# Hymba layer on one core: the zero rows beside the decode tokens written to DRAM ahead of time

## The chip, the cores and the metric

The kernel runs on one core of a Trainium2 chip. The metric is the device time of one execution in microseconds, the median of several runs.

## The reference

One layer of a hybrid decoder in its inference step, in float32, for 2,048 prompt tokens (one sequence) and 8 decode tokens (one of each of 8 sequences), with a model width of 2,048. What is computed, cut to what matters:

```python
shift, scale, gate = adaln(c, w_c, b_c)
h = rmsnorm(x, g_pre) * (1.0 + scale) + shift
u_a, v_a, z_a, x_b, z_b = split(h @ w_in)              # five parts of 1024 columns
y_a = u_a * chunk_mix(layernorm(v_a), w_s, b_s) * silu(z_a)
y_b, h_re, h_im = s5_branch(x_b, h0, ...)              # diagonal state-space scan, 64 groups of 16 channels
y_b = y_b * silu(z_b)
out = x + gate * rmsnorm(concat([y_a, y_b]) @ w_out, g_post)
```

The outputs are `out` for prompt and decode tokens, the decode tokens' normalised `v_a`, and the S5 states of both.

## The kernel before, in words

**Arithmetic.** Every large matrix product is made of three float32 products on TensorE (`mm3`, lines 97 to 99): operand and weight are each split into a high and a low part, and high-high, high-low and low-high are summed. A weight piece of 128 x 1024 is loaded by SyncE (`wraw`, L108), ScalarE casts its high half (`whi`, L90), and VectorE or GpSimd subtracts to get the low half (`wlo`, L85). Weights are loaded one column tile ahead.

**Tiles and stages.** Tokens go in four blocks `b` of 512 (the last has the 8 decode tokens besides, in two ranges of 256 and 264 tokens, `ranges`, L58). In the first part every block computes 16 column tiles of 128 columns: 8 of `x_b` and 8 of `z_b`, with 16 steps of k each. The loop over blocks (L1449 to L1470) starts a block with `group_start`, which makes the normalised input of the block from x, its row factor `R` and the shift (L373 to L375), and goes on with `phase1_rest` (L570), which calls `half(i, hf)` before each half of a column tile. `half` advances generators by a step: the statistics of the next block (`stats`: an x load L329, two squares on ScalarE L335 and L337, an addition on GpSimd L338, sixteen times two k tiles, and then `rms_wide`, which gives `R` by a Newton iteration on VectorE, L140 to L145), the matrices of the S5 branch (`s5_mats`: GpSimd products L810 to L812 for E, F and `bb`, ScalarE casts such as `qh` L883, transposes and small products on TensorE), and the gate of the ada layer (L271 to L291). The accumulators of the column tiles are PSUM tiles `acc`, in a ring of four banks.

**The stores that the change is about.** The results of a column tile `e` go to DRAM in chunks of 8 tokens, time-major, for the S5 scan that follows: `XB[e]` has for each of 128 columns, 8 times `t` and 2 halves (high, low) a row of 272 numbers, `ZB[e]` for each `t` and column a row of 264. The 256 prompt chunks lie in the middle, the 8 decode sequences beside them: in front (`0:ND`) and at the end (`ND+NK:XW`) of `XB`'s rows, and at the end of `ZB`'s. A decode token fills one of the eight times; the other seven are zero. `ev_xb` (L391 to L415) and `ev_zb` (L417 to L432) evict a tile, and in the last block write the decode part too: GpSimd sets a tile `dz` to zero (L409, L429), VectorE (and ScalarE in `ev_zb`) writes the token's numbers into it (L412, L413, L430, L431), and SyncE stores the whole, zeros and all (L414, L415, L432). Each number row of 8 float32 is a packet of 32 B: 2,048 packets for each of the two `XB` stores of a tile, 1,024 for the `ZB` store. `dz` has two buffers.

**What sets the order.** The code is written in the order of the loops above, and a scheduler that simulates the engines then sets the order on each engine; so a transfer need not stand where the loop yields it. Each engine, SyncE's queue of transfers among them, works in its order.

Of the kernel before, what the change touches and what calls it, by code (L numbers as in the profile page):

```python
# [11 lines left out]
F32 = mybir.dt.float32  # L12
F32R = mybir.dt.float32r
I32 = mybir.dt.int32
AF = mybir.ActivationFunctionType
# [6 lines left out]
ND = 8  # L22
# [5 lines left out]
G = 64  # L28
# [3 lines left out]
TC = 8  # L32
NK = L // TC
XW = NK + 2 * ND
HW = NK + ND
EPS = 1e-6
NE = 8
# [20 lines left out]
def ranges(b):  # L58

    return [(0, TB)] if b < NB - 1 else [(0, 256), (256, 264)]  # L60


class Builder:
# [330 lines left out]
    def ev_xb(self, b, e, acc):  # L394

        hi, lo = self.tile_(), self.tile_()
        hv, lv = (o[:, 0:TB].rearrange("p (t k) -> p t k", t=TC) for o in (hi, lo))
        for a, (r0, rn) in zip(acc, ranges(b)):
            m = min(rn, TB - r0)
            av = a[:, 0:m].rearrange("p (k t) -> p t k", t=TC)  # L400
            ks = slice(r0 // TC, (r0 + m) // TC)
            self.S.copy(hv[:, :, ks].bitcast(F32R), av)
            self.sub(self.V, lv[:, :, ks].bitcast(F32R), av, hv[:, :, ks])
        cols = slice(ND + b * 64, ND + b * 64 + 64)
        self.SP.dma_start(self.XB[e][:, :, 0, cols], hv)
        self.SP.dma_start(self.XB[e][:, :, 1, cols], lv)
        if b == NB - 1:
            dz = self.sp_.tile([128, 2, TC, 2, ND], F32, tag="dz", bufs=2, name=self.nm("dz"))
            self.G.memset(dz, 0.0)  # L409
            d = acc[1][:, 256:264]  # L410
            for i, t in ((0, TC - 1), (1, 0)):
                self.V.tensor_copy(dz[:, i, t, 0, :].bitcast(F32R), d)  # L412
                self.sub(self.V, dz[:, i, t, 1, :].bitcast(F32R), d, dz[:, i, t, 0, :])  # L413
            self.SP.dma_start(self.XB[e][:, :, :, 0:ND], dz[:, 0])  # L414
            self.SP.dma_start(self.XB[e][:, :, :, ND + NK : XW], dz[:, 1])  # L415

    def ev_zb(self, b, e, acc):  # L417
        o = self.tile_()
        ov = o[:, 0:TB].rearrange("p (t k) -> p t k", t=TC)
        for a, (r0, rn) in zip(acc, ranges(b)):  # L420
            m = min(rn, TB - r0)
            av = a[:, 0:m].rearrange("p (k t) -> p t k", t=TC)
            os_ = ov[:, :, r0 // TC : (r0 + m) // TC]
            self.S.activation(os_, av, AF.Sigmoid)
            self.V.tensor_mul(os_, os_, av)
        self.SP.dma_start(self.ZB[e].rearrange("t p k -> p t k")[:, :, b * 64 : b * 64 + 64], ov)
        if b == NB - 1:
            dz = self.sp_.tile([128, 2, TC, ND], F32, tag="dz", bufs=2, name=self.nm("dz"))
            self.G.memset(dz[:, 0], 0.0)  # L429
            self.S.activation(dz[:, 0, 0, :], acc[1][:, 256:264], AF.Sigmoid)  # L430
            self.V.tensor_mul(dz[:, 0, 0, :], dz[:, 0, 0, :], acc[1][:, 256:264])  # L431
            self.SP.dma_start(self.ZB[e].rearrange("t p k -> p t k")[:, :, NK:HW], dz[:, 0])  # L432

    def ev_v(self, b, j, acc):
        T, V, S = self.T, self.V, self.S
# [941 lines left out]
    def build(self):  # L1377
        nc, tc, I, V, G, SP = self.nc, self.tc, self.I, self.V, self.G, self.SP
# [29 lines left out]
        with tc.manual_schedule():  # L1408
            w, acc = self.startup(st, NG, nta)
# [19 lines left out]
        def mats_step():  # L1429

            paced[0] += 1
            while paced[1] * n_a < paced[0] * (8 * NE + 2):
                paced[1] += 1
                next(mats, None)
        def stats(b):

            n = blk(b)
            ssq = self.xp.tile([128, TB + ND], F32, tag="ssq", bufs=1, name=self.nm("ssq"))
            for i in range(KT):
                self.stat_add(self.xp, self.xload(self.xp, "xst", b, i, 2), ssq, i, n, G)  # L1440
                yield 1
            self.rms_wide(ssq, n, self.R[b])
            if n > TB:
                self.hdec(self.R[b])
        pair = lambda ntl: lambda hf: [self.wsplit(self.wpair(I["win"], ntl[1][0], 0))] if hf else []
        half1 = lambda ntl, i: lambda hf: self.wsplit(self.whalf(I["win"][ntl[1][i]], hf))


        for b in range(NB):  # L1449
            st_ = stats(b + 1) if b + 1 < NB else iter(())  # L1450
            if b:
                w = self.group_start(b, nta, w[0], self.R[b], half1(nta, 2))
            def half(i, hf, b=b, st_=st_):
                if i >= 3:
                    next(st_, None)
                if b == 0 and i == 8 and hf == 0:
                    self.s5_lanes(pp)
                if (b or i > 8) and i < len(nta[0]) - 1:
                    mats_step()
                if b and hf:  # L1460
                    next(gate, None)
                return (), ()
            w = self.phase1_rest(b, nta, 2 if b else NG, half, w, pair(nta) if b + 1 < NB else half1(ntb, 0))
            for _ in st_:
                pass
# [20 lines left out]
        for b in (NB - 1, *range(NB - 1)):  # L1486
            if b < NB - 1:
                w = self.v_tokens(b, w[0], self.R[b], half, ntb[1][8])
            if b != NB - 2:
                w = self.phase1_rest(b, ntb, 8 if b < NB - 1 else 0, half, w, lambda hf: [self.vpair(0)] if hf else [])  # L1490
            else:
                y0, ws0 = [], []
                raws = []
                def last(k):

                    if k == 1:
                        raws.extend(self.wraw(self.wpair(I["wout"], g, 0)) for g in (0, 2))
                    if k in (9, 14):
                        ws0.extend(self.wpieces(raws.pop(0)))
                    if k >= 4 and k % 2 == 0:  # L1500
                        y0.append(self.yload(0, len(y0)))
                self.phase1_rest(b, ntb, 8, half, w, lambda hf: [], last)
# [94 lines left out]
```

## Time and profile before

| | |
|---|---|
| median of 3 runs | 2885.63 us |
| lowest, highest | 2882.94, 2888.16 us |
| the profiled execution's own time | 2882.97 us |
| its span, first to last instruction | 2880.9 us |
| mean granted TensorE clock | 0.994 |
| busy share of VectorE, ScalarE, GpSimd | 55%, 37%, 36% |
| DRAM traffic | 466.94 MB read, 102.66 MB written |

The profile shows one execution on the core. Times are from the span's start. Block 0's column tiles run until about 270 us, blocks 1 and 2 until about 690, and block 3, where the decode part is stored, from about 690 to 900 us. The rest of the time goes to the v, z, u tiles, the S5 scan and the output projection, which the change does not touch.

### The profile page before, as it was taken

To read this page: it belongs to the slowest core of one execution; us is meant where nothing else is said; L and a number is where in the kernel's file an instruction comes from. 1 tells how busy PE (TensorE), PEld (TensorE's weight loads), DVE (VectorE), ACT (ScalarE), POOL (GpSimd) and SP (SyncE) were. 2 spreads that over 40 slices of the span, in tenths; PEclk is the share of its full clock that TensorE was granted. 3 is DMA by queue.
4 is the path that set the end of the run, shared out by engine and by line. 5 is a ranking of instruction groups with operands and counts; after the bars stand their busy time and mean duration, and the time that the engine had idled before them with its cause. 6 is when DMAs were issued, how large, how long until landed. Compare 5 with 4: busy or idle time off the path is not lost.

```text
span 2880.9 us, 44125 instructions
## 1 busy us (share of the span) xinstructions
PE 2817.2 (98%) x15708; PEld 2365.8 (82%) x15708; DVE 1570.4 (55%) x2907; ACT 1062.2 (37%) x2008; POOL 1048.5 (36%) x973
## 2 busy tenths in 40 slices
PE   7999999999999999999999999999999999999998
PEld 4676777778899999988888888888888888888976
DVE  4467656465342837564647545573641273472866
ACT  3334444334233232423233332433243333434543
POOL 1128562662431233323232323233334355263442
PEclk9999999999999999999999999999999999999999
DMA  9898997987987373847475656646573355464676
GB/s 363 287 250 230 265 261 229 282 234 210 198 209 207 106 236 125 267 131 223 133 245 185 180 174 196 209 145 208 159 229 106 112 178 171 132 219 126 197 235 221
DMA packets 455167, 581.20 MB, mean 202 GB/s; under 512 B 216609, under 2 KB 303265, under 8 KB 454945
## 3 DMA queue, kind: packets, MB, share of 16 engines
q1 hardware_dynamic: 454946, 578.38, 66.9%
q8 instruction: 123, 2.02, 0.3%
q14 instruction: 98, 0.80, 0.1%
HBM read 466.94 MB, written 102.66 MB: 198 GB/s over the span
## 4 chain that ended last, share of the span: by engine, by line
PE 73%; DVE 14%; DMA 6%; issue 3%; POOL 1%; SPq 1%; ACT 1%; DVEq 0%; ACTq 0%; POOLq 0%
PE acc L97 21%; PE acc L99 20%; PE acc L98 20%; DVE Ub L943 3%; DVE wlo L85 2%; PE acc L655 2%; PE acc L656 2%; PE acc L657 2%; PE ada L271 1%; DMA wraw<-in_win 1%; DVE Ub L954 1%; DVE sct L953 1%; DVE sct L951 1%; DVE Ub L952 1%; DMA wraw<-in_woutr 1%
## 5 line engine op out<-in xcount | busy, mean ns | idle before, releaser
L85 DVE TENSOR_TENSOR wlo<-wraw,whi 128x512 fp32r<-128x512 f32 x626 | 544.6, 878 | 832.9 <-ACT whi L90 811.8
L90 ACT CAST whi<-wraw 128x512 fp32r<-128x512 f32 x960 | 580.4, 620 | 1101.3 <-PE acc L98 634.8
L97 PE MATMUL acc<-hi,whi 128*128 128x512 f32 (+2 forms) x2816 | 979.2, 349 | 1.4 <-ACT vtok L663 0.8
L99 PE MATMUL acc<-hi,wlo 128*128 128x512 f32 (+2 forms) x2816 | 968.7, 344 | 4.0 <-DVE wlo L85 3.9
L98 PE MATMUL acc<-lo,whi 128*128 128x512 f32 (+2 forms) x2816 | 968.2, 344 | 3.8 <-DVE lo L375 3.5
L85 POOL TENSOR_TENSOR wlo<-wraw,whi 128x512 fp32r<-128x512 f32 x334 | 472.7, 1418 | 1025.0 <-ACT whi L90 911.8
L97 PEld LDWEIGHTS acc<-hi,whi 128*128 128x128 f32 x2816 | 531.1, 189 | 82.2 <-issue 14.0
L99 PEld LDWEIGHTS acc<-hi,wlo 128*128 128x128 f32 x2816 | 530.4, 188 | 74.0 <-DVE wlo L85 6.1
L98 PEld LDWEIGHTS acc<-lo,whi 128*128 128x128 f32 x2816 | 531.1, 189 | 65.0 <-DVE lo L375 6.7
L97 PE MATMUL acc<-yhi,whi 128*128 128x512 f32 (+1 forms) x1024 | 377.3, 369 | 3.8 <-DVE o L1118 2.8
L99 PE MATMUL acc<-yhi,wlo 128*128 128x512 f32 (+1 forms) x1024 | 375.5, 368 | 2.1 <-POOL wlo L85 2.1
L98 PE MATMUL acc<-ylo,whi 128*128 128x512 f32 (+1 forms) x1024 | 376.1, 368 | 0.0
L97 PEld LDWEIGHTS acc<-yhi,whi 128*128 128x128 f32 x1024 | 193.5, 189 | 39.6 <-DVE o L1118 3.6
L99 PEld LDWEIGHTS acc<-yhi,wlo 128*128 128x128 f32 x1024 | 193.0, 189 | 36.7 <-POOL wlo L85 2.7
L98 PEld LDWEIGHTS acc<-ylo,whi 128*128 128x128 f32 x1024 | 193.5, 189 | 34.5 <-issue 0.7
L656 PE MATMUL acc<-wlo,hi 128*128 128x512 f32 x384 | 151.4, 394 | 0.0
L657 PE MATMUL acc<-whi,lo 128*128 128x512 f32 x384 | 151.1, 394 | 0.0
L655 PE MATMUL acc<-whi,hi 128*128 128x512 f32 x384 | 148.6, 394 | 0.0
L943 DVE SCALAR_TENSOR_TENSOR Ub<-Ub,apow 128x128 f32<-128x128 f32 (+6 forms) x384 | 146.3, 447 | 2.3 <-ACT Ub L930 2.0
L1032 POOL TENSOR_TENSOR sg<-sg,zbl 128x264 f32<-128x264 f32 x64 | 54.9, 858 | 195.5 <-DVE sg L1031 115.3
L90 ACT CAST hh<-hr 128x264 fp32r<-128x264 f32 x64 | 26.5, 414 | 194.6 <-DMA hr<-Ub 92.2
L1121 POOL TENSOR_TENSOR ossq<-ossq,osq 128x512 f32<-128x512 f32 (+1 forms) x60 | 81.5, 1358 | 35.3 <-ACT osq L1114 35.1
(295 smaller groups left out, 3137.6 us busy)
## 6 DMA issues: line engine op xcount, KB each, us to landing
wraw<-in_win SPq DMA_DIRECT2D x272, 512.0 KB
wraw<-in_wout SPq DMA_DIRECT2D x128, 512.0 KB
xr<-XB SPq DMA_DIRECT2D x128, 272.0 KB
x<-in_xT SPq DMA_DIRECT2D x128, 256.0 KB
wraw<-in_wss SPq DMA_DIRECT2D x64, 512.0 KB
wraw<-in_winv SPq DMA_DIRECT2D x48, 512.0 KB
XB<-t SPq DMA_DIRECT2D x64, 256.0 KB
wraw<-in_wgt SPq DMA_DIRECT2D x32, 512.0 KB
```

The source lines that it names most:

```text
L85: eng.tensor_tensor(out, a, b, op=ALU.subtract)
L90: self.S.copy(hi, raw)
L97: mm(acc, whi, xhi, start=start, stop=False)
L98: mm(acc, whi, xlo, start=False, stop=False)
L99: mm(acc, wlo, xhi, start=False, stop=stop)
L271: self.T.matmul(ps[k * 32 : k * 32 + 32, 0:256], self.stat[:, q * 4 + k, :], raw[:, k * 256 : k * 256 + 256], start=q == 0, stop=q == 3)
L655: mm(acc[c], hh, wh, start=k == 0, stop=False)
L656: mm(acc[c], hh, wl, start=False, stop=False)
L657: mm(acc[c], ho, wh, start=False, stop=k == KT - 1)
L943: V.scalar_tensor_tensor(o, i, f, o, op0=ALU.mult, op1=ALU.add)
L1032: self.G.tensor_tensor(sg, sg, zb, op=ALU.mult)
L1121: eng.tensor_tensor(ssq[:, 0:nn], ssq[:, 0:nn], sq[:, 0:nn], op=ALU.add)
```

## The change

The tile `dz` shrinks to the token's own numbers, one row for high and one for low (and one for `ZB`), so no memset is needed, and the token's numbers are computed once and not twice. The last block's stores write these rows alone: 256 packets of 32 B for each of the two `XB` stores, 128 for `ZB`'s. The zeros come from a tile `zt` that GpSimd sets to zero once; `zero_rows` yields 24 transfers out of it, for each `e` two of 1,792 packets to `XB` and one of 896 to `ZB`. From block 1 on, `half` takes one of them per half column tile.

```diff
--- before.py
+++ after.py
@@ -405,14 +405,23 @@
         self.SP.dma_start(self.XB[e][:, :, 0, cols], hv)
         self.SP.dma_start(self.XB[e][:, :, 1, cols], lv)
         if b == NB - 1:
-            dz = self.sp_.tile([128, 2, TC, 2, ND], F32, tag="dz", bufs=2, name=self.nm("dz"))
-            self.G.memset(dz, 0.0)
+            dz = self.sp_.tile([128, 2, ND], F32, tag="dz", bufs=2, name=self.nm("dz"))
             d = acc[1][:, 256:264]
-            for i, t in ((0, TC - 1), (1, 0)):
-                self.V.tensor_copy(dz[:, i, t, 0, :].bitcast(F32R), d)
-                self.sub(self.V, dz[:, i, t, 1, :].bitcast(F32R), d, dz[:, i, t, 0, :])
-            self.SP.dma_start(self.XB[e][:, :, :, 0:ND], dz[:, 0])
-            self.SP.dma_start(self.XB[e][:, :, :, ND + NK : XW], dz[:, 1])
+            self.V.tensor_copy(dz[:, 0, :].bitcast(F32R), d)
+            self.sub(self.V, dz[:, 1, :].bitcast(F32R), d, dz[:, 0, :])
+            self.SP.dma_start(self.XB[e][:, TC - 1, :, 0:ND], dz)
+            self.SP.dma_start(self.XB[e][:, 0, :, ND + NK : XW], dz)
+
+    def zero_rows(self, z):
+
+        z = z.rearrange("p (t h n) -> p t h n", t=TC, h=2)
+        for e in range(NE):
+            self.SP.dma_start(self.XB[e][:, 0 : TC - 1, :, 0:ND], z[:, 1:])
+            yield
+            self.SP.dma_start(self.XB[e][:, 1:TC, :, ND + NK : XW], z[:, 1:])
+            yield
+            self.SP.dma_start(self.ZB[e].rearrange("t p k -> p t k")[:, 1:TC, NK:HW], z[:, 1:, 0, :])
+            yield
 
     def ev_zb(self, b, e, acc):
         o = self.tile_()
@@ -425,11 +434,10 @@
             self.V.tensor_mul(os_, os_, av)
         self.SP.dma_start(self.ZB[e].rearrange("t p k -> p t k")[:, :, b * 64 : b * 64 + 64], ov)
         if b == NB - 1:
-            dz = self.sp_.tile([128, 2, TC, ND], F32, tag="dz", bufs=2, name=self.nm("dz"))
-            self.G.memset(dz[:, 0], 0.0)
-            self.S.activation(dz[:, 0, 0, :], acc[1][:, 256:264], AF.Sigmoid)
-            self.V.tensor_mul(dz[:, 0, 0, :], dz[:, 0, 0, :], acc[1][:, 256:264])
-            self.SP.dma_start(self.ZB[e].rearrange("t p k -> p t k")[:, :, NK:HW], dz[:, 0])
+            dz = self.sp_.tile([128, ND], F32, tag="dzz", bufs=2, name=self.nm("dz"))
+            self.S.activation(dz, acc[1][:, 256:264], AF.Sigmoid)
+            self.V.tensor_mul(dz, dz, acc[1][:, 256:264])
+            self.SP.dma_start(self.ZB[e][0, :, NK:HW], dz)
 
     def ev_v(self, b, j, acc):
         T, V, S = self.T, self.V, self.S
@@ -1446,6 +1454,9 @@
         half1 = lambda ntl, i: lambda hf: self.wsplit(self.whalf(I["win"][ntl[1][i]], hf))
 
 
+        zt = self.sp_.tile([128, TC * 2 * ND], F32, name="zt")
+        G.memset(zt, 0.0)
+        zeros = self.zero_rows(zt)
         for b in range(NB):
             st_ = stats(b + 1) if b + 1 < NB else iter(())
             if b:
@@ -1455,6 +1466,8 @@
                     next(st_, None)
                 if b == 0 and i == 8 and hf == 0:
                     self.s5_lanes(pp)
+                if b:
+                    next(zeros, None)
                 if (b or i > 8) and i < len(nta[0]) - 1:
                     mats_step()
                 if b and hf:
```

Instructions are moved by the scheduler. The first place is SyncE's order at the end of the loads for the S5 matrices, in the middle of block 0. A name's number counts tiles and differs by a few between the kernels (`x_1455` before is `x_1457` now). Before:

```order
L108 DMA wraw_3002<-in_wgt 128x1024
L108 DMA wraw_3103<-in_wgt 128x1024
L108 DMA wraw_1838<-in_win 128x1024
L108 DMA wraw_1890<-in_win 128x1024
L108 DMA wraw_1953<-in_win 128x1024
L808 DMA dd_2508<-in_dcol 32x2
L329 DMA x_1455<-in_xT 128x512
L329 DMA x_1493<-in_xT 128x512
```

Now (two pieces of one stretch of 32 rows):

```order
L419 DMA XB_57<-zt 128x14x8
L421 DMA XB_57<-zt 128x14x8
L108 DMA wraw_3006<-in_wgt 128x1024
L423 DMA ZB_65<-zt 128x7x8
L419 DMA XB_58<-zt 128x14x8
L108 DMA wraw_3109<-in_wgt 128x1024
L421 DMA XB_58<-zt 128x14x8
...
L419 DMA XB_64<-zt 128x14x8
L421 DMA XB_64<-zt 128x14x8
L423 DMA ZB_72<-zt 128x7x8
L329 DMA x_1457<-in_xT 128x512
L329 DMA x_1495<-in_xT 128x512
```

All 24 transfers out of `zt` stand between the weight loads here, and ahead of the x loads of block 1's statistics; none stands in block 1.

The second place is ScalarE's order behind that, where `x_1455` (now `x_1457`) is squared and column tile 6 is evicted (`t_1532<-acc_1453`, now `t_1534<-acc_1455`). Before:

```order
L90 CAST whi_1840<-wraw_1838 128x512
L335 ACTIVATE ssq_1454<-x_1455 128x512
L337 ACTIVATE t_1495<-x_1493 128x512
L402 CAST t_1532<-acc_1453 128x512
L90 CAST whi_1844<-wraw_1838 128x512
L90 CAST whi_1892<-wraw_1890 128x512
L90 CAST whi_1896<-wraw_1890 128x512
```

Now:

```order
L90 CAST whi_1846<-wraw_1840 128x512
L90 CAST whi_1894<-wraw_1892 128x512
L90 CAST whi_1898<-wraw_1892 128x512
L852 COPY sc_1951<-pC_1946 128x128
L90 CAST whi_1957<-wraw_1955 128x512
L90 CAST whi_1961<-wraw_1955 128x512
L335 ACTIVATE ssq_1456<-x_1457 128x512
L337 ACTIVATE t_1497<-x_1495 128x512
L402 CAST t_1534<-acc_1455 128x512
```

The eviction stands behind the two squares in both; but casts of weight pieces that used to follow the eviction (`whi_1844` to `whi_1896`, now `whi_1846` to `whi_1898`), and two of the next load, now stand ahead of the squares.

The third place is GpSimd's order around the additions to block 1's sum of squares (L338; `E`, `F`, `bb`, `mu` and `sc` belong to the S5 matrices). The GpSimd lines 810 to 812 are 818 to 820 in the changed kernel. Before:

```order
L811 TENSOR_TENSOR E_2243<-E_2243,mu_2236 128x256
L810 TENSOR_TENSOR bb_2921<-sl_cre,sb_2505 128x32 x2
L338 TENSOR_TENSOR ssq_1454<-ssq_1454,t_2339 128x512
L810 TENSOR_TENSOR mu_2236<-sc_2255,pw 128x576
L338 TENSOR_TENSOR ssq_1454<-ssq_1454,t_2401 128x512
L812 TENSOR_TENSOR F_2353<-F_2353,mu_2236 128x576
L868 TENSOR_SCALAR sc_2255<-sc_2255 128x128
```

Now:

```order
L820 TENSOR_TENSOR E_2932<-E_2932,mu_2925 128x256
L818 TENSOR_TENSOR mu_2925<-bb_2924,pw 128x2x128
L819 TENSOR_TENSOR E_2932<-E_2932,mu_2925 128x256
L338 TENSOR_TENSOR ssq_1456<-ssq_1456,t_2234 128x512
L338 TENSOR_TENSOR ssq_1456<-ssq_1456,t_2297 128x512
L338 TENSOR_TENSOR ssq_1456<-ssq_1456,t_2341 128x512
L338 TENSOR_TENSOR ssq_1456<-ssq_1456,t_2403 128x512
L881 MEMSET bd_3002 128x128
L884 COPY bd_3002<-bb_2924 64x4x16 x2
```

Before, these are the last two additions, and the rest of the second F (`F_2353`) and the third E (`E_2929`) follow them. Now the last four additions stand in a row behind the rest of the second F and the third E (`E_2932`). Counted from the first `bb` product (`bb_1929`, now `bb_1931`), ten additions follow before and fifteen now.

## Rows read from the trace of the kernel before

**Rows 1.** Busy time of each engine, from the page

```profile
PE 2817.2 (98%) x15708; PEld 2365.8 (82%) x15708; DVE 1570.4 (55%) x2907; ACT 1062.2 (37%) x2008; POOL 1048.5 (36%) x973
```

**Rows 2.** Timeline of TensorE, block 3: start us, us, operation [idle before <-releaser]

```profile
778.74 1.02 PE L282 MATMUL adat<-sel,t 128*128 128x9 f32 x4 [3.97 <-DVE t L275]
...
815.49 0.39 PE L99 MATMUL acc<-hi,wlo 128*128 128x256 f32 x1 [2.22 <-DVE wlo L85]
...
816.32 0.36 PE L97 MATMUL acc<-hi,whi 128*128 128x264 f32 x1 [0.44 <-DVE dz L431]
```

**Rows 3.** Windows: us, PE PEld DVE ACT POOL busy, PEclk, DMA share, GB/s

```profile
778.70:785.50 6.80, 6.76 (x36) 6.76 (x37) 2.46 (x6) 1.64 (x5) 4.47 (x10) 0.60 0.82 213
```

**Rows 4.** GpSimd: a memset in the timeline, and who waited (us, times) for dz

```profile
766.88 0.31 POOL L409 MEMSET dz<- 128x256 f32 x1 [15.12 <-DMA XB<-dz]
...
  POOL dz L409: 43.3, 6
```

**Rows 5.** Timeline of ScalarE, block 3

```profile
774.20 0.62 ACT L883 CAST qh<-F 128x512 fp32r<-128x512 f32 x1 [11.54 <-POOL F L812]
```

**Rows 6.** Timeline of SyncE (issues of transfers), block 0

```profile
168.21 0.91 SPq L108 DMA_DIRECT2D wraw<-in_wgt  x2
169.21 1.60 SPq L108 DMA_DIRECT2D wraw<-in_win  x3
...
173.08 6.78 SPq L329 DMA_DIRECT2D x<-in_xT  x10
```

**Rows 7.** Windows in block 0, and one of 32 B packets in block 3

```profile
140.00:200.00 60.00, 60.00 (x267) 47.23 (x266) 44.05 (x157) 18.26 (x33) 10.43 (x12) 0.97 0.99 254
172.00:176.40 4.40, 4.40 (x18) 3.55 (x17) 4.21 (x31) 0.00 (x0) 0.00 (x0) 0.63 1.00 382
733.00:734.00 1.00, 1.00 (x11) 1.00 (x10) 0.17 (x1) 0.00 (x0) 0.00 (x0) 1.00 0.73 51
```

**Rows 8.** Timeline of SyncE, block 3: the first of three dz issues, and what follows them

```profile
712.17 1.24 SPq L415 DMA_DIRECT2D XB<-dz  x1
...
716.54 5.66 SPq L907 DMA_DIRECT2D MT<-ks  x8
```

**Rows 9.** The tile dz: ns from issue to landing, least, median and most

```profile
L415 SPq DMA_DIRECT2D XB<-dz x8: 945/2324/3102, 712.2 to 801.1; - x8
```

**Rows 10.** Timeline of ScalarE, block 0

```profile
178.65 0.63 ACT L335 ACTIVATE ssq<-x 128x512 f32<-128x512 f32 x1 [0.64 <-DMA x<-in_xT]
179.22 0.63 ACT L337 ACTIVATE t<-x 128x512 f32<-128x512 f32 x1
179.76 0.56 ACT L402 CAST t<-acc 128x512 fp32r<-128x512 f32 x1
```

**Rows 11.** Timeline of VectorE, block 0

```profile
181.90 0.68 DVE L85 TENSOR_TENSOR t<-acc,t 128x512 fp32r<-128x512 f32 x1
...
203.18 0.19 DVE L785 TENSOR_TENSOR sl_cre<-sl_t,sl_den 128x32 f32<-128x32 f32 x1
```

**Rows 12.** Timeline of TensorE, block 0

```profile
189.62 0.50 PE L97 MATMUL acc<-hi,whi 128*128 128x512 f32 x1
```

**Rows 13.** Timeline of GpSimd, block 0

```profile
203.45 0.50 POOL L810 TENSOR_TENSOR bb<-sl_cre,sb 128x32 f32<-128x32 f32 x2 [5.32 <-DVE sl_cre L785]
...
243.53 1.30 POOL L338 TENSOR_TENSOR ssq<-ssq,t 128x512 f32<-128x512 f32 x1
244.78 1.43 POOL L812 TENSOR_TENSOR F<-F,mu 128x576 f32<-128x576 f32 x1
...
257.81 0.81 POOL L811 TENSOR_TENSOR E<-E,mu 128x256 f32<-128x256 f32 x1
```

**Rows 14.** VectorE and TensorE at the start of block 1

```profile
268.36 0.69 DVE L145 SCALAR_TENSOR_TENSOR R<-t,R 128x512 f32<-128x512 f32 x1
...
269.57 5.38 DVE L373 SCALAR_TENSOR_TENSOR x<-x,GT,R 128x512 f32<-128x512 f32 x8
...
275.67 0.50 PE L98 MATMUL acc<-lo,whi 128*128 128x512 f32 x1 [1.42 <-DVE lo L375]
```

## The prediction

> **What bounds the kernel now.** I read the page's busy table first: TensorE is busy 97.8% of the span [rows 1], so the time moves only by what TensorE waits for, or by its clock. The timeline of TensorE in block 3, where the old stores are made, gives the waits that the change can touch: 3.97, 2.22 and 0.44 us idle, all released by VectorE [rows 2]. The windows by stage show the second price of such a wait: after the first of them the granted clock is 0.60 over 6.80 us [rows 3], between the levels of 1.2 and 2.4 GHz. Then I followed the releaser of the longest wait back through GpSimd and ScalarE [rows 4, 5], and last read the stretch from 168 to 270 us, where the changed order puts the zero transfers. Each of the two places is priced by its own stage.
>
> **What goes in block 3 (the gain).** The GpSimd memset of `dz` at 766.88 us stood idle 15.12 us for a transfer out of the same buffer; in all, such waits before L409 are 43.3 us, 6 times [rows 4]. GpSimd works in order, so the F products queue behind it; ScalarE's cast `qh` waited 11.54 us for F [rows 5]; ScalarE's weight casts queue behind `qh`, VectorE's `wlo` and `t` behind those, and TensorE waits 3.97 us at 778.74 [rows 2]. With no memset this whole chain starts earlier. Sum: 3.97 + 2.22 + 0.44 us of idle, and (1 - 0.60) x 6.80 = 2.7 us of clock, 9.3 us. Less follows if a late weight takes the place of the late F; the shortest of it that I accept is the first wait alone, 4.0 us. I take 9.3, since the old transfers that delayed the weights there leave as well: per pair 2 x 2,048 + 1,024 packets of 32 B become 2 x 256 + 128, so 35,840 of 40,960 packets leave the stage. The sixteen fewer pairs of small VectorE operations cost or give nothing: VectorE is at 55% [rows 1], and weight splitting covers them. If that cover were gone they would be a few us spread over 90 us.
>
> **What comes at 168 us (the loss).** The 35,840 packets do not vanish. The generator yields one transfer per half column tile, but the order of instructions on SyncE shows all 24 among the weight loads and ahead of `x_1457`, the first x load of block 1's statistics. SyncE reached that place at 168.21 us, issued five weight loads by 170.8 and then ten x loads [rows 6].
>
> The price of a zero transfer. No row of before shows it, so nearest rows bound it. Low: in a stretch with almost nothing but such packets the engines moved 51 GB/s [rows 7], 1,600 packets of 32 B per us, so 35,840 take 22.4 us. Middle: three issues of 2,048 packets with no other between them (L415, L414, L415) take from 712.17 to the next issue at 716.54, 1.46 us each [rows 8]; a zero transfer of 1,792 then takes 1.27 us, one of 896 takes 0.64, and 16 x 1.27 + 8 x 0.64 = 25.5 us. High: from issue to landing, the median of L415 is 2,324 ns [rows 9], which if nothing overlapped gives 2.03 and 1.02, so 40.7 us. I take 25.5, from the rows of back-to-back transfers, which these are. Below the low end I see nothing, except that a gap in which the queues idle could cover part.
>
> The Trainium skill's page DMA: Bandwidth & Descriptors (Anatomy of one DMA) gives a fixed cost of about 2.0 us to each DMA on GpSimd's path, mostly waiting for the receipt of the write. Taken for these, which SyncE issues, and end to end, it would make 24 transfers at least 48 us and the net loss 22 us more than my sum; the 1.46 us between neighbours [rows 8] speak against it, being below one such fixed cost.
>
> What waits for it. A weight of 512 KB takes 1.37 us at the 382 GB/s of 172 to 176.4 us [rows 7]; an x load takes 6.78 / 10 = 0.68 us [rows 6]. From 168.21, five weights and one x end at 175.7; ScalarE squared that x at 178.65 [rows 10], a lag of 2.9 us. With 25.5 us of zeros ahead the same sum gives 204.1 us for `x_1457` and 204.8 for `x_1495`. In the old order ScalarE's next operation there, the eviction L402 of column tile 6, came at 179.76 and VectorE's subtraction at 181.90 [rows 10, 11]. In the new order the eviction still stands behind the two squares: 204.8 + 0.63 + 0.56 + 0.68 = 206.7 us until tile 6's accumulator bank is free. The accumulators have four banks; tile 10 takes that bank, and TensorE's rows put its start 24 matmuls behind 189.62 [rows 12], at 60.00 / 267 = 0.225 us each [rows 7], so at 195.0. TensorE then stands 11.7 us. With as much for the clock after it as in block 3 (2.7 us): 14.4 us.
>
> The other path is the statistics R of block 1. In before GpSimd's last addition of a square ends at 244.83, 41.4 us after it took up `bb` at 203.45 [rows 13], which waits for VectorE at 203.18 [rows 11] and does not move. In the new order five more of the 1.30 us additions (6.5 us) and the F and E products that stood from 244.78 to 258.62 (13.8 us) come ahead of it: 203.45 + 41.4 + 6.5 + 13.8 = 265.2, 20.3 us later. R ended at 269.05 and block 1's inputs (L373) began at 269.57, with TensorE waiting for them [rows 14]. Between last addition and R lie 24.2 us in which VectorE's steps of R alternate with weight pieces that wait for TensorE, so part of the 20.3 is given back there; the floor is TensorE's own 14.4. I take 16 us as the loss, close to that floor. The ends: with 22.4 us of zeros the stall is 3.1 us shorter, and 40.7 makes it 15.2 longer, so 11.3 to 29.6; below 11.3 only if the eviction does not wait.
>
> **Sum.** 2882.97 + 16.0 - 9.3 = 2889.7 us for the profiled execution. That one lies 2.66 us under the median of the runs shown, so 2892.3 on the median, +6.7. A measurement can tell about 0.2%, 5.8 us.
>
> **Rivals.**
> (1) **No change to speak of**: the zeros take the low price or the eviction slips ahead of part of them, the loss is 8 to 13 us and the gain 9.3: net -1 to +4, 2885 to 2889. For it: the low price rests on a measured rate. Against: the order leaves no x load ahead of the zeros.
> (2) **Faster**: the zeros are hidden. The two places compete for one thing, whether the accumulator bank is late; with four banks there are 195.0 - 182.6 = 12.4 us of slack already. If the transfers run beside the loads, or the x loads land before 192.6 us, TensorE does not stand, and if R's later start is given back in its 24.2 us to the last 3 us, the net is -9.3 to -6, 2876 to 2880; it decides at 12 us of delay, under half of my 25.5. For it: the loads reach 382 GB/s [rows 7], and engines that took loads and zeros in turn would land an x load early. Against: one queue, SyncE's, issues both, the 20.3 us of GpSimd's order remain, and in the window at 733 us such packets went no faster than 51 GB/s [rows 7].
> (3) **Much slower**: every transfer costs its issue-to-landing time, 40.7 us of zeros: stall 26.9 + 2.7 = 29.6, net +20.3, 2906. For it: [rows 9]. Against: [rows 8]. The page's fixed cost, named above, points this way; by it alone the time would be near 2915 us.
> That the change would spread the transfers, as its loop says, I exclude by the order.
>
> **Chances.** Forecast 0.44, of which 0.33 lie over +5.8 us and 0.11 at or below; rival 1 0.26; rival 2 0.20; rival 3 0.10. So faster 0.20, same 0.37, slower 0.43. The range leaves out the better part of rival 2's gain below 2878 and the upper half of rival 3 above 2907.
>
> **What the profile would show.** Right: 24 zero transfers issued from about 168 us, 25 us of DMA at near 50 GB/s; L335 of the first x near 204 us; TensorE idle some 12 us near 195 us, released by VectorE's `t`, with a reduced clock after it; R some 16 us later than 269; in block 3 no memset row, no idle of 4 us at the `adat` matmuls and a clock near 1.00 after them. Wrong: x landing before 193 us, a stall that is given back before block 1, or block 3 waiting for a weight in the place of F.

## The result, and the profile after

The changed kernel takes 2898.16 us (median of 6 runs, 2895.59 to 2903.17), the kernel before 2883.52 us in the 6 runs beside them. The ratio is 1.0052, 95% interval 1.0040 to 1.0064: slower by 15.0 us by the ratio, 11.5 to 18.5. The forecast was slower by 6.7.

SyncE's timeline of the changed kernel shows the 24 transfers where the order put them:

```profile
167.09 0.40 SPq L419 DMA_DIRECT2D XB<-zt  x1
167.53 0.69 SPq L421 DMA_DIRECT2D XB<-zt  x1
168.27 1.08 SPq L108 DMA_DIRECT2D wraw<-in_wgt  x1
...
198.56 1.92 SPq L423 DMA_DIRECT2D ZB<-zt  x1
200.57 5.80 SPq L329 DMA_DIRECT2D x<-in_xT  x10
```

From the first of them to the x loads pass 33.5 us; in before it was 4.9 us from the first weight load to the x loads [rows 6], so the zeros took 28.6 us. Then ScalarE's and VectorE's timelines, the rows that answer to [rows 10, 11]:

```profile
204.34 0.63 ACT L335 ACTIVATE ssq<-x 128x512 f32<-128x512 f32 x1 [3.06 <-DMA x<-in_xT]
206.12 0.63 ACT L337 ACTIVATE t<-x 128x512 f32<-128x512 f32 x1 [1.15 <-DMA x<-in_xT]
206.65 0.57 ACT L402 CAST t<-acc 128x512 fp32r<-128x512 f32 x1
...
266.68 1.33 ACT L337 ACTIVATE t<-x 128x512 f32<-128x512 f32 x2 [5.19 <-DMA x<-in_xT]
```

```profile
207.25 0.69 DVE L85 TENSOR_TENSOR t<-acc,t 128x512 fp32r<-128x512 f32 x1 [3.18 <-ACT t L402]
...
293.47 0.67 DVE L145 SCALAR_TENSOR_TENSOR R<-t,R 128x512 f32<-128x512 f32 x1
294.18 3.85 DVE L373 SCALAR_TENSOR_TENSOR x<-x,GT,R 128x512 f32<-128x512 f32 x4
```

GpSimd's last additions to the sum of squares, which answer to [rows 13]:

```profile
261.60 2.67 POOL L338 TENSOR_TENSOR ssq<-ssq,t 128x512 f32<-128x512 f32 x2
267.46 2.64 POOL L338 TENSOR_TENSOR ssq<-ssq,t 128x512 f32<-128x512 f32 x2 [3.18 <-ACT t L337]
```

They end at 270.1 us, and R at 294.1 us, 25.1 us later than before [rows 14]. The two squares that they wait for stand behind their own x loads, the last two of block 1's statistics. SyncE issued these at 227.55 us in before and at 260.84 us in the changed kernel:

```profile
227.55 1.22 SPq L329 DMA_DIRECT2D x<-in_xT  x2
```

```profile
260.84 1.09 SPq L329 DMA_DIRECT2D x<-in_xT  x2
```

TensorE's timeline has its two stalls, the accumulator's at 208 us and a second at the start of block 1:

```profile
208.00 0.80 PE L97 MATMUL acc<-hi,whi 128*128 128x512 f32 x1 [13.35 <-DVE t L85]
...
296.23 0.69 PE L861 MATMUL pT<-c_ident,E 128*128 128x128 f32 x2 [8.58 <-POOL E L820]
...
298.67 0.69 PE L861 MATMUL pT<-c_ident,E 128*128 128x128 f32 x2 [0.90 <-POOL E L819]
...
301.43 1.08 PE L271 MATMUL ada<-wraw,cstat 128*32 128x256 f32 x8 [2.07 <-DMA wraw<-in_wgt]
303.60 0.79 PE L98 MATMUL acc<-lo,whi 128*128 128x512 f32 x1 [1.09 <-DVE lo L375]
```

The windows (columns as in [rows 3]) show the transfers and the weights between them at 113 GB/s. The clock falls behind both stalls, to 0.78 and 0.54. In block 3 TensorE has no wait left:

```profile
167.00:200.50 33.50, 27.65 (x131) 22.22 (x129) 22.42 (x122) 3.42 (x7) 1.88 (x2) 0.94 0.85 113
...
208.00:220.00 12.00, 12.00 (x43) 9.63 (x44) 5.50 (x5) 3.84 (x8) 11.31 (x20) 0.78 1.08 326
...
296.00:310.00 14.00, 9.71 (x36) 5.41 (x37) 13.94 (x16) 5.61 (x10) 9.71 (x11) 0.54 0.77 212
...
700.00:900.00 200.00, 200.00 (x1707) 194.32 (x1706) 94.37 (x183) 71.24 (x165) 62.79 (x84) 1.00 0.78 207
```

The same window of before, with the 6.80 us of [rows 3] in it, has TensorE idle for 6.64 us and the clock at 0.98:

```profile
700.00:900.00 200.00, 193.36 (x1642) 187.85 (x1641) 80.42 (x170) 62.76 (x149) 64.44 (x100) 0.98 0.87 205
```

**The lag curve.** Where the time goes is best seen by comparing progress: each kernel here has the same 13,056 weight loads of accumulating matmuls on TensorE, and the lag is the time at which the n-th begins, less the same in before, both counted from the first of them. The table has the growth of that lag from one point to the next; the points are those that before reached at 183, 260, 377, 691 and 828 us.

| kernel (ratio of times) | to 183 | 183-260 | 260-377 | 377-691 | 691-828 | to the end |
|---|---|---|---|---|---|---|
| changed (1.0052) | 0.0 | 14.1 | 11.2 | -0.1 | -9.8 | -1.3 |
| e3 burst only (1.0089) | 1.6 | 14.5 | 10.9 | 0.0 | 4.6 | -1.3 |
| e9 order kept (1.0017) | 4.1 | 1.8 | 10.9 | 2.4 | -9.8 | -2.1 |
| e8 merged (1.0024) | 4.1 | 10.6 | 10.8 | 0.0 | -9.8 | -6.4 |
| e13 burst, old order (1.0072) | 3.7 | 26.5 | 0.7 | 0.0 | -9.8 | 2.6 |
| e12, three times as long (1.0266) | 0.0 | 82.8 | 0.4 | -0.1 | -9.9 | 4.7 |
| e15 after x (0.9995) | -0.4 | -0.5 | 9.4 | -0.1 | -9.8 | -3.0 |
| e1 spread (0.9989) | -0.1 | -0.4 | 4.7 | 7.1 | -9.8 | -1.1 |
| e10 zeros in block 3 (1.0013) | 0.0 | 0.2 | -0.3 | 0.0 | 7.4 | 0.5 |
| e6 three dz buffers (0.9998) | 3.1 | -0.6 | -0.1 | 0.0 | 1.8 | 0.1 |
| e11 late (0.9980) | 3.1 | -0.6 | -0.3 | 0.0 | -9.8 | 1.8 |
| e14 late, in the scan (0.9979) | 0.0 | 0.0 | -0.3 | 0.0 | -9.8 | 7.6 |

The first and the last column scatter by some us, also where two kernels do the same there; the middle ones repeat to 0.1 or 0.3 us. So the changed kernel loses 14.1 us at the end of block 0's S5 loads, 11.2 us more at the start of block 1, and gains 9.8 us in block 3.

The lag at 377 us, the sum of the first three columns, can be set beside the start of block 1. Counted in the same way, block 1's inputs (L373) begin 25.4 us late in the changed kernel, 27.1 in e3, 16.9 in e9, 25.7 in e8 and 30.9 in e13; the lags at 377 us are 25.3, 27.0, 16.8, 25.5 and 30.9. In these five kernels the loss up to there is thus as large as the lateness of R, whatever part of it TensorE has lost before. The rows of VectorE in e9 and in e13:

```profile
285.79 7.75 DVE L373 SCALAR_TENSOR_TENSOR x<-x,GT,R 128x512 f32<-128x512 f32 x8
```

```profile
301.21 5.38 DVE L373 SCALAR_TENSOR_TENSOR x<-x,GT,R 128x512 f32<-128x512 f32 x8
```

### The profile page after: what moved, and what is told of

Its sections match the earlier page's. It is cut to its first block, busy times and chain, and to the rows that moved or that the text cites. A ratio compares the mean times of both kernels' runs of the same rounds, so it can differ in the third digit from the quotient of the medians.

```text
span 2894.6 us, 44109 instructions
## 1 busy us (share of the span) xinstructions
PE 2817.6 (97%) x15708; PEld 2366.8 (82%) x15708; DVE 1576.0 (54%) x2891; ACT 1064.9 (37%) x2008; POOL 1048.9 (36%) x958
## 4 chain that ended last, share of the span: by engine, by line
PE 79%; DVE 11%; DMA 5%; issue 2%; SPq 1%; ACT 1%; POOL 1%; DVEq 0%; ACTq 0%; POOLq 0%
PE acc L97 22%; PE acc L99 22%; PE acc L98 22%; DVE Ub L951 3%; DVE wlo L85 2%; PE ada L271 1%; PE acc L663 1%; PE acc L664 1%; PE acc L665 1%; DMA x<-in_xT 1%; DVE Ub L962 1%; DVE sct L961 1%; DVE sct L959 1%; PE mix L539 1%; DMA wraw<-in_woutr 1%
## 5 line engine op out<-in xcount | busy, mean ns | idle before, releaser
L85 DVE TENSOR_TENSOR wlo<-wraw,whi 128x512 fp32r<-128x512 f32 x626 | 554.7, 893 | 863.3 <-ACT whi L90 821.2
L97 PE MATMUL acc<-hi,whi 128*128 128x512 f32 (+2 forms) x2816 | 981.1, 349 | 14.1 <-DVE t L85 13.3
L90 ACT CAST hh<-hr 128x264 fp32r<-128x264 f32 x64 | 26.5, 414 | 192.7 <-DMA hr<-Ub 93.5
```

What stands on the lines that cost most here:

```text
L85: eng.tensor_tensor(out, a, b, op=ALU.subtract)
L90: self.S.copy(hi, raw)
L97: mm(acc, whi, xhi, start=start, stop=False)
```

## The experiments

The first theory was the prediction's: burst and order make the loss, the stores that left block 3 make the gain. The rivals were that packets cost the same anywhere, that order alone or transfers alone make the loss, and that GpSimd's memset makes the gain.

**e1_spread.** Zeros tied to block 1's evictions (the same in `ev_zb` for `ZB`, and no `zero_rows`); `zero_tile` is a VectorE product of the evicted tile's first 112 columns with 0:

```diff
+        if b == 1:
+            z = self.zero_tile(hi)
+            self.SP.dma_start(self.XB[e][:, 0 : TC - 1, :, 0:ND], z)
+            self.SP.dma_start(self.XB[e][:, 1:TC, :, ND + NK : XW], z)
```

> The changed kernel, but the zeros can't be issued early: in block 1 VectorE makes a small zero tile out of each evicted column tile (times 0), and the two XB transfers or the ZB transfer of zeros leave with that tile, so the same 35,840 packets are spread over some 190 us. The order of block 0 is that of the kernel before. Theory (the loss is the burst at 167 to 200 us together with the order that it brings; block 3 gains 11 us): no stall near 195 us, R of block 1 back near 269 us, 2870 to 2876 us, 8 to 13 us under before. Rival (the packets cost their 25 us wherever they stand): 2893 to 2900 us, as the changed kernel.

Measured: ratio 0.9989 (0.9980 to 0.9999), 2884.58 us against 2886.60. The lateness at 183 to 260 us is gone and block 3's gain is there, but 11.8 us are lost in block 1, where TensorE now waits, and the clock is 0.93 in the window from 360 to 460 us (timeline of TensorE):

```profile
371.94 0.99 PE L282 MATMUL adat<-sel,t 128*128 128x9 f32 x4 [2.14 <-DVE t L275]
...
432.63 0.52 PE L158 MATMUL ssum<-sqh,ones 128*128 128x512 f32 x1 [3.63 <-ACT sqh L90]
```

Neither side was right: spread out, the packets cost less than half of the burst's loss, but not nothing.

**e3_burst_only.** Kernel before with the change's `zero_rows`, its tile and its call; the old stores of the last block stay.

```diff
+        zt = self.sp_.tile([128, TC * 2 * ND], F32, name="zt")
+        G.memset(zt, 0.0)
+        zeros = self.zero_rows(zt)
...
+                if b:
+                    next(zeros, None)
```

> The kernel before with the 24 zero transfers added, the last block's stores as they were (zeros are written twice). TensorE's order is that of the changed kernel in every row. Theory (loss in blocks 0 and 1 of 25 us, gain in block 3 of 11 us, independent of each other): 2906 to 2912 us, 25 us over before. Rival (the prediction's loss of 16 us, the rest of the lag made good later on): 2897 to 2901 us.

Measured: ratio 1.0089 (1.0075 to 1.0102), 2913.96 us, 25.7 us by the ratio. The theory's 25 us hold, and the rival's give-back does not come: the two steps, 14.5 and 10.9 us, are those of the changed kernel, and stay to the end. In block 3 the profiled execution loses 4.6 us more, which was not taken apart.

**e6_dz3.** One number, in both lines that make a `dz` tile (one is shown):

```diff
-            dz = self.sp_.tile([128, 2, TC, 2, ND], F32, tag="dz", bufs=2, name=self.nm("dz"))
+            dz = self.sp_.tile([128, 2, TC, 2, ND], F32, tag="dz", bufs=3, name=self.nm("dz"))
```

> The kernel before with three dz buffers in place of two, nothing else: the memsets of GpSimd wait less for the stores, all 40,960 packets stay in block 3. Theory (the gain of block 3 is GpSimd's wait for the buffer, and F behind it): the idle of 4 us at the adat matmuls goes, 2875 to 2879 us. Rival (the gain comes from the packets that leave SyncE's queue, so that weights land earlier): within 2 us of before.

Measured: 0.9998 (0.9989 to 1.0008). This tells nothing of the theory, since the wait did not go: with a third buffer the memsets stand earlier in GpSimd's order and still wait (timeline of GpSimd):

```profile
767.82 0.32 POOL L409 MEMSET dz<- 128x256 f32 x1 [14.78 <-DMA XB<-dz]
```

**e9_order_kept.** Zeros spread as in e1, and cheap transfers in the place of the burst:

```diff
+        for e in range(NE):
+            self.SP.dma_start(self.DUM[e][:, 0, 0:384], z[:, 0:384])
+            yield
+            self.SP.dma_start(self.DUM[e][:, 1, 0:384], z[:, 0:384])
+            yield
+            self.SP.dma_start(self.DUM[e][:, 2, 0:192], z[:, 0:192])
+            yield
```

> Zeros spread over block 1 as in the spread kernel, and in the place of the 24 early transfers 24 others into an unused DRAM tile, of 1,536 or 768 B per partition in one packet each: 3,072 packets, 3.9 MB, some 10.3 us at the 382 GB/s of the loads, against 25 us. GpSimd's, ScalarE's and TensorE's order in blocks 0 and 1 is close to the changed kernel's (64 of TensorE's rows differ, 496 between before and changed). Theory (the transfers' time is the cause): x lands near 189 us, no stall of TensorE near 195 us, part of R's lateness left by the order, 2873 to 2883 us. Rival (the changed order is the cause, the transfers matter little): 2893 to 2900 us.

Measured: 1.0017 (1.0006 to 1.0029), 2892.10 us against 2886.60, above the theory's range and just under the rival's. The x loads come 13.2 us later than before on SyncE, counted as above; TensorE has no wait for an accumulator behind them, and the first step is 1.8 us only. But the second step is 10.9 us, as large as with the whole burst. The zeros spread over block 1 do not make it, since the first of them goes out at 332.78 us and L373 stands at 285.79. So the size of that step does not follow the transfers' time.

**e10_zeros_b3.** As e1, with `b == NB - 1` in the place of `b == 1` and six zero tiles.

> The changed kernel with its small token stores, but the zeros go out in block 3 beside them, from tiles that VectorE makes (column tile times 0, six buffers), so all 40,960 packets are in block 3 again and GpSimd has no memset to wait for. Order of blocks 0 to 2 as before. Theory P (block 3's gain of 11 us comes from the packets that leave its queue): within 3 us of before, TensorE again idle some 4 us near 778 us. Theory M (the gain comes from GpSimd's memset, which waited 15 us for a buffer): 8 to 11 us under before.

Measured: 1.0013 (1.0004 to 1.0022), 7.4 us lost in block 3 against before and 17.2 against the changed kernel. No `dz` memset is left, and yet TensorE waits at the same place, longer than before [rows 2]. The timelines of TensorE, of ScalarE, of GpSimd and of SyncE in this kernel:

```profile
781.61 1.02 PE L282 MATMUL adat<-sel,t 128*128 128x9 f32 x4 [6.64 <-DVE t L275]
```

```profile
762.05 1.14 ACT L90 CAST whi<-wraw 128x512 fp32r<-128x512 f32 x2 [11.81 <-DMA wraw<-in_win]
...
777.07 0.62 ACT L893 CAST qh<-F 128x512 fp32r<-128x512 f32 x1 [12.01 <-POOL F L822]
```

```profile
775.17 0.52 POOL L911 MEMSET ks<- 64x512 f32 x1 [8.10 <-DMA MT<-ks]
```

```profile
758.81 4.34 SPq L409 DMA_DIRECT2D XB<-zt  x1
763.20 2.11 SPq L410 DMA_DIRECT2D XB<-zt  x1
...
766.75 6.43 SPq L917 DMA_DIRECT2D MT<-ks  x8
```

F is as late as in [rows 5], because GpSimd now waits for other transfers (`MT`), which stand behind the zeros on SyncE, and ScalarE waits for a weight. So theory P holds in its main point: with the packets back and no memset the gain of block 3 is gone. The loss against before is 3.8 us by the ratio (1.2 to 6.3), where P had at most 3. VectorE's zero tiles (0.2 us each, 16 times) and transfers of their own for the zeros are in this kernel besides, and which of them makes the 7.4 us in block 3 is open.

**e11_late.** Only tile 0's zeros in block 1; the others while the S5 step of the tile before runs:

```diff
+        if e + 1 < NE and gl < 3:
+            z = self.zero_tile(x[:, 0].bitcast(F32))
+            if gl == 0:
+                self.SP.dma_start(self.XB[e + 1][:, 0 : TC - 1, :, 0:ND], z)
...
```

> The changed kernel, but the zeros of tile e + 1 go out while the S5 step of tile e runs (from 900 us on, where the DMA engines are busy 0.58 of the time, 0.92 in block 1); those of tile 0 in block 1. Tied there by a small VectorE product. Theory (35,840 packets cost about 11 us in every stage of the first part, which is full of loads, and nothing where the queues have room): 870 to 874 of the last digits, that is 2871 to 2876 us or 10 to 13 us under before. Rival (they hold up the S5 step's own loads): within 3 us of before.

Measured: 0.9980 (0.9969 to 0.9992), 2878.36 us against 2885.39, 5.8 us by the ratio, faster than both kernels. Block 3's 9.8 us are kept and the first part loses nothing; the size expected was 10 to 13, since 4 us go lost at 1056 to 1070 us, where TensorE waited for a load of the S5 step (timeline of TensorE):

```profile
1052.87 0.36 PE L97 MATMUL pu<-xr,pr 128*128 128x264 f32 x1 [0.99 <-DMA pr<-PS]
...
1061.75 0.37 PE L97 MATMUL pu<-xr,pr 128*128 128x264 f32 x1 [2.53 <-DMA pr<-PS]
```

**e14_late_scan.** The same zeros sent from `s5_scan`, one transfer at each of the first three levels.

```diff
+            if e + 1 < NE and lv < 3:
+                self.zeros_next(e + 1, lv, self.zero_tile(Ub[:, 0, 0, :]))
```

> As the late kernel, but the zeros of tile e + 1 go out during the scan of tile e, some 40 us later, and not during the loads at the start of its step, where the late kernel's TensorE waited 0.99 and 2.53 us for a load (pr) and lost 4 us against before between 1056 and 1070 us. Theory: those 4 us are not lost, 2873 to 2878 us on a median of before of 2885, 9 to 12 us under before. Rival (the waits were chance): as the late kernel, 7 us under.

Measured: 0.9979 (0.9968 to 0.9991), 6.1 us under before by the ratio, the same as e11 and short of the theory's 9 to 12. The 4 us at 1060 were not lost, but 7.6 us were between 828 us and the end in the profiled execution. By the lag of all of TensorE's weight loads, 6.6 of them go between 1200 and 2000 us, where these zeros still go out. There TensorE waits for the S5 step in rows that before does not have, 3.2 us in all; what the rest is was not taken apart (TensorE's waits in this stretch of e14: us, times, longest):

```profile
PE pg L1045 <- ACT hh L90: 2.4, 3, 1.0
...
PE pg L1045 <- DMA wr<-MQ: 0.8, 2, 0.6
```

**e12_burst_order_before** and **e13_burst_sized.** Onto e11, at the burst's place, transfers that the scheduler takes for cheap, of 128 x 140 packets of 4 B each (in e13 of 128 x 44):

```diff
+        for e in range(2):
+            self.SP.dma_start(self.DUM[e][:, :, 0:1], z.rearrange("p (a b) -> p a b", b=1))
+            yield
```

> The late kernel, plus two transfers of 17,920 packets of 4 B each into an unused DRAM tile at the place on SyncE where the changed kernel has its zeros, just ahead of the five weight loads. The scheduler takes them for cheap, so 476 of the 496 changed rows of TensorE stay as before, GpSimd's additions too. Theory (burst and order cost each about half of the 25 us): 11 to 16 us over the late kernel, a stall of TensorE near 195 us. Rival (transfers alone make all of it): 25 us over the late kernel. Rival (order alone): 0 to 4 us.

> The late kernel, plus two transfers of 5,632 packets of 4 B each into an unused DRAM tile at the changed kernel's place on SyncE, ahead of the weight loads. The former kernel of this kind had 35,840 packets of 4 B, which took about 80 us; 11,264 should take 25 us, as long as the changed kernel's zeros. 480 of the 496 changed rows of TensorE stand as in the kernel before. Theory (the burst is paid once, by the stall in block 0; the lateness at the start of block 1 belongs to the changed order): a lag of 13 to 20 us after block 0 that does not grow by more than 4 us at the start of block 1; 12 to 18 us over the late kernel. Rival (a burst of this length makes R late by itself): the lag grows by 8 to 12 us at the start of block 1; 22 to 27 us over.

Measured: e12 1.0266 (1.0252 to 1.0280), far over all that was expected, because 4 B packets are dearer than 32 B packets: the x loads came 81.7 us later than before on SyncE. e13, sized by that, delayed them by 27.1 us, as the changed kernel's burst: 1.0072 (1.0054 to 1.0090), 2906.58 us, 26.5 us over e11 by the two ratios. The size is that of the rival, but the course is the theory's: 26.5 us come at once, and the start of block 1 adds 0.7 us (0.4 in e12). The old order does not make the burst cheaper: at 377 us this kernel is 30.9 us behind, the changed kernel 25.3. Here all five weight loads stand behind the burst, and TensorE waits for a weight and not for an accumulator (timeline of TensorE in e13):

```profile
208.64 0.80 PE L97 MATMUL acc<-hi,whi 128*128 128x512 f32 x1 [14.47 <-ACT whi L90]
...
225.72 0.50 PE L99 MATMUL acc<-hi,wlo 128*128 128x512 f32 x1 [2.93 <-DVE wlo L85]
...
243.88 0.69 PE L869 MATMUL pT<-c_ident,E 128*128 128x128 f32 x2 [5.20 <-POOL E L828]
```

**e8_merged.** The changed kernel; where a row's end and the next row's start meet in DRAM, one packet (`i` is `3 * XW - ND`; beside it go two transfers of three rows, and `ZB`'s):

```diff
+            m = x[:, i : i + 11 * XW].rearrange("p (r k) -> p r k", k=XW)
+            self.SP.dma_start(m[:, :, 0 : 2 * ND], z)
```

> The changed kernel, with the 8 zeros at the end of one XB row and the 8 at the start of the next, which lie side by side in DRAM, written as one packet of 64 B: 24,576 packets and 32 transfers for 35,840 and 24, the same bytes, early as in the changed kernel (64 of TensorE's rows stand otherwise). If a packet has a price whatever its size, the burst is 31% shorter (about 8 us) and the stall at 208 us is 4 to 7 us and not 13; 2888 to 2894 us. If bytes set the price: within 2 us of the changed kernel.

Measured: 1.0024 (1.0014 to 1.0033), 2892.38 us, as the price by the packet has it. On SyncE the x loads come 18.7 us late and not 28.6, and TensorE's stall is 4.11 us (its timeline in e8):

```profile
203.24 0.79 PE L97 MATMUL acc<-hi,whi 128*128 128x512 f32 x1 [4.11 <-DVE t L85]
```

The second step is 10.8 us all the same.

**e15_after_x.** The changed kernel with `zt` made from the last x tile of block 1's statistics:

```diff
-        G.memset(zt, 0.0)
...
+                if b == 1 and i == KT - 1:
+                    self.V.tensor_single_scalar(self.zt, x[:, 0 : TC * 2 * ND], 0.0, op=ALU.mult)
```

> The changed kernel, but VectorE makes the zero tile from the last x tile of block 1's statistics (times 0), so the 24 transfers can't be issued before that load has landed, some 215 us; they follow from there to the start of block 1, and the order before them is that of the kernel before. Theory (what is lost is the lateness of the x loads, near one for one: 28.6 us later on SyncE made 25.7 us at L373 in the changed kernel, 13.2 made 15.2 with cheaper transfers in their place): block 1's inputs within 4 us of before, little of the 25 us at the start of block 1, the rest of the price, up to 11 us as in the spread kernel, in the weights of early block 1; 2876 to 2886 us. Rival (the burst costs its 25 us wherever it falls in the first part): 2895 to 2900 us.

Measured: 0.9995 (0.9986 to 1.0005), 2883.52 us: the changed kernel's 15 us are gone. The zeros now lie between 232 and 290 us, block 1's inputs (L373) begin at 270.49 us against 269.57 [rows 14], and what is lost is 9.4 us just behind, about what the packets cost in e1. The theory's time came, its rule did not: x lateness does not pass on one for one, since e9 and the changed kernel have nearly the same second step with 13.2 and 28.6 us of it.

## Why the prediction was right, and where its sizes and a cause were not

The forecast's sign, its place and its two terms stand; the size is more than twice the forecast's, 15.0 us for 6.7, because the loss was put too low. Step by step:

- **The place of the transfers** held: all 24 from 167 us, ahead of the x loads.
- **Their price** was 28.6 us in place of 25.5, inside the bounds of 22.4 and 40.7. The upper bound was misread: the times of [rows 9] are lengths of the issues on SyncE, one behind the other as in [rows 8], and not times to landing, which the trace does not give for them. The sign "near 50 GB/s" did not come either, since weights went between the zeros (113 GB/s). The Trainium skill's page DMA: Bandwidth & Descriptors (Anatomy of one DMA) gives about 2.0 us of fixed cost to a DMA of GpSimd's path; an estimate from it, end to end, would have been 48 us here. The measured 28.6 / 24 = 1.19 us per transfer, from SyncE's queue, does not agree with such a sum.
- **The stall** went as worked out: first square at 204.34 us (204.1 forecast), eviction done at 207.9 (206.7), TensorE idle 13.35 us (11.7), clock loss (1 - 0.78) x 12 = 2.6 us (2.7). Together that is 16.0 us; of it 14.1 are left in the lag at 260 us (14.4), so this match is closer than its parts.
- **The step that fell short is the other path: "I take 16 us as the loss, close to that floor".** The prediction had the last addition end at 265.2 us by GpSimd's order, 20.3 us late, and 4.3 us of that given back on the way to R. Measured, the last addition ended at 270.1 us, 4.9 us later still, because ScalarE's last squares waited for their x loads. And nothing was given back: from the last addition to R it is 24.0 us, and was 24.2 before. 16.0 + 4.9 + 4.3 = 25.2 us; R is 25.1 us late, and the lag at 377 us is 25.3.
- **What belongs to the order** the runs separate in part. e9, e8, e3 and the changed kernel have the new order, x loads 13.2, 18.7, 28.2 and 28.6 us late, and all the same 10.8 to 11.2 us more at the start of block 1; e12 and e13, with the old order, have 0.4 and 0.7 us there. So that step goes with the new order and not with the length of the burst. No kernel has the new order without early transfers, so it is not shown that the order alone would cost 11 us. Which engine's order carries it (GpSimd's additions behind the E and F products, TensorE's moved `pT` and `pK`, or SyncE's, which issued the last x loads 33.3 us later) was not taken apart.
- **The gain** was 9.8 us where 9.3 was forecast, but its cause was named wrongly. The prediction gave it to GpSimd's memset and took the packets as a help; e10 has no memset of `dz`, has the packets, and has the wait. The memset waited for the queue as others did, and others wait in its place. The other half, the memset kept and the packets gone, was not run.

The sum was 16.0 - 9.3 = 6.7; with the measured steps it is 25.3 - 9.8 = 15.5 us to 828 us, 14.0 to the end of the profiled execution, and 15.0 by the runs. The rivals "no change" and "faster" fell because 28.6 us are far more than the slack, which was there: e9's x loads came 13.2 us late and TensorE did not wait for an accumulator. The "much slower" price of 40.7 us did not come.

## What to carry to other kernels

Here the scheduler put work that depended on nothing into the middle of block 0, while the loop yields it in block 1. Tie such work by a data dependency to the stage where the queue really has room (here the S5 steps), as the late kernels do. Price a moved transfer by its packets and by the loads queued behind it, and look at the order of the other engines too, since here a step of 11 us went with the order and not with the length of the burst. If a change seems to pay by removing an instruction that waits, put its queue's load back without the instruction, and see which of the two was the cause.

## What the runs showed of the hardware that was not expected

A small packet had a price of its own and not by its bytes. The burst of 35,840 packets of 32 B delayed the x loads by 28.6 us, 0.80 ns a packet; e8's 24,576, of which 11 in 24 were of 64 B, by 18.7 us, 0.76 ns. Packets of 4 B were three times as dear: 27.1 us for 11,264 in e13 and 81.7 us for 35,840 in e12, 2.4 and 2.3 ns each. SyncE's rows of e12 show the two transfers and the weight loads stuck behind them:

```profile
167.92 38.21 SPq L422 DMA_DIRECT2D DU<-zt  x2
206.18 42.62 SPq L108 DMA_DIRECT2D wraw<-in_wgt  x2
```
